# Attention scores with the low part of k on 128 partitions, and longer planned load times, in a one-core transformer block

## The chip, the cores and the metric

One core of one Trainium2 chip runs the whole kernel, one launch. The metric is the device time of that launch in microseconds. The engines are TensorE (PE, with its weight loads as PEld), VectorE (DVE), ScalarE (ACT), GpSimd (POOL) and SyncE (SP), which issues the DMAs.

## What is computed

One layer of a streaming encoder on x of 1024 x 1024: a first gated feed-forward block, a mixing block with two branches (differential attention with 8 heads, an mLSTM with 4 heads), a second feed-forward block, a final norm. The change lies in the attention branch:

```python
def diff_attention(q, k, v, lam, g_subln, lambda_init):
    q = rope(q); k = rope(k)                       # 8 heads, 2 components c, 64 wide
    s = einsum('bqhcd,bkhcd->bchqk', q, k) * Dh ** -0.5   # by blocks of 128 queries
    p = softmax(where(key_chunk <= query_chunk, s, -inf))
    a = p[:, 0] - lam * p[:, 1]
    o = einsum('bhqk,bkhd->bqhd', a, v)
    return rmsnorm(o, g_subln) * (1.0 - lambda_init)
```

## The kernel before

All matmuls are made of float32r parts: a number is split into a high part, the float32r rounding (a cast on ScalarE), and a low part, the rest (a subtraction on VectorE). A product is high x high, high x low and low x high: three matmuls (`mm3`, lines 264 to 266). Weights come in units of 128 x 1024 (512 KB): a DMA into a raw buffer, the cast to `wh` on ScalarE, the subtraction to `wl` on VectorE.

The stages follow each other: first feed-forward block; projections; mLSTM and attention (attention from some 1200 to 1880 us), both with dense projections put between their steps; merge; second feed-forward block.

In the attention stage the head's q, k and v come back from DRAM. `Q` holds the high part of q in partitions 0 to 63 and the low part in 64 to 127. `Kh` holds the high part of k in both halves, so one matmul over 128 rows gives (q high + q low) x k high (line 1551). `Kl` holds the low part of k in partitions 0 to 63, and the second matmul, over 64 rows, gives q high x k low into the same bank (line 1552). There are 192 such pairs: for 8 heads, 2 components and 8 blocks of queries, in pieces of up to 512 keys. Each head is loaded in four quarters j (`load`, lines 1499 to 1510): two DMAs for `Q`, two for `Kh`, one for `Kl`. `Kh` and `Kl` have one buffer, so a head's K is asked for when the head before has all its scores.

The order of the stage is planned by the class `Flow` (lines 55 to 152), a small event simulation that runs while the program is built. Work comes as generators. A step "P" is work on TensorE with a planned cost, "A" one on ScalarE, "D" one on VectorE; "wait" lets planned time pass, "take" and "give" hold buffers, "need" and "set" are flags. Each instruction is written into its engine's list at the moment that the plan reaches it, and each engine works through its list in order. Where no step for TensorE is ready, `chunk` gives a piece of dense work: projections of q and k (`qp`, `job_qk`), of gates (`gp`, `job_g`) and of the mLSTM's output (`ab`, `job_b`). A matmul of scores is planned by `sc_time` (line 1533): 0.227 us for 512 columns, 0.12 for 256, for both matmuls of a pair.

A load is planned as a "wait" between its issue and the step that uses it. `self.lead` (line 165) is that time for a unit of weights (`unit_ahead`, lines 242 to 259: raw buffer, DMA, wait, cast, subtraction, raw buffer free; two raw buffers), for the inputs of the output projections (`load_y`, line 1205) and for a head's normed output (`merged`, line 1695). `loads` waits 3.0 for the first quarter of a head and 1.0 for each other, `loads_v` 3.5 for v. Other planned times, as the 6.0 for stores of rotated q and k, stay out of the change.

Of the kernel before, what the change touches and what calls it, by code (L numbers as in the profile page):

```python
# [11 lines left out]
F32 = mybir.dt.float32  # L12
# [31 lines left out]
class Halves:  # L44


    def __init__(self, tiles):
        self.tiles = tiles
# [105 lines left out]
class Net:  # L154
    def __init__(self, ctx, tc, aps, dbg):
        self.ctx, self.tc, self.nc, self.a, self.dbg = ctx, tc, tc.nc, aps, dbg
        nc = self.nc
        e = ctx.enter_context
        self.const = e(tc.tile_pool(name="const", bufs=1))
        self.wraw = e(tc.tile_pool(name="wraw", bufs=2))  # L160
        self.whl = e(tc.tile_pool(name="whl", bufs=4))
        self.up = e(tc.tile_pool(name="up", bufs=1))
        self.tmp = e(tc.tile_pool(name="tmp", bufs=6))
        self.uid = 0
        self.flow, self.lead = None, 5.0
        c = self.const
        self.vec = c.tile([P, NVEC], F32, name="vec")
        nc.sync.dma_start(out=self.vec, in_=aps["vec"])
        self.ones = c.tile([P, P], F32, name="ones")
        nc.vector.memset(self.ones, 1.0)  # L170
        self.zeros = c.tile([P, 64], F32, name="zeros")
        nc.gpsimd.memset(self.zeros, 0.0)
        self.onz = c.tile([P, 16], F32, name="onz")
        nc.vector.memset(self.onz, 0.0)
        nc.vector.memset(self.onz.rearrange("p (a b) -> p a b", b=2)[:, :, 0:1], 1.0)
        self.ident = c.tile([P, P], F32, name="ident")
        make_identity(nc, self.ident)
        self.epsc = c.tile([P, 1], F32, name="epsc")
        nc.vector.memset(self.epsc, EPS)
        self.mod = [c.tile([P, 8], F32, name=f"mod{g}") for g in range(9)]  # L180
        self.sc = [c.tile([P, 8], F32, name=f"sc{g}") for g in range(3)]
        self.new_u()
# [1009 lines left out]
    def load_y(self, n, src):  # L1192
        nc = self.nc
        ns = slice(n * NW, n * NW + NW)
        if n not in self.y:
            self.y[n] = [[self.u_tile(c, k, n) for c in "hl"] for k in range(KT)]
        done = []
        for k in range(KT):
            hi, lo = self.y[n][k]
            nc.sync.dma_start(out=lo.bitcast(F32), in_=src[k][:, ns])  # L1200
            if self.flow is None:
                self.split_in(hi, lo)
            else:
                def chain(k=k, hi=hi, lo=lo):
                    yield "wait", self.lead + 0.7 * k
                    yield "A", 0.62, lambda: nc.scalar.copy(hi, lo.bitcast(F32))
                    yield "D", 0.69, lambda: nc.vector.tensor_sub(lo, lo.bitcast(F32), hi.bitcast(F32))
                    if k == KT - 1:
                        done.append(1)
                self.flow.spawn(self.flow.now, chain())  # L1210
        return done if self.flow is not None else [1]
# [274 lines left out]
    def stage_attn(self, dense):  # L1486
        nc, tc = self.nc, self.tc
        nlam, gcol = self.lam[:, 2:3], self.lam[:, 3:4]
        with tc.tile_pool(name="a1", bufs=1) as a1, tc.tile_pool(name="a2", bufs=2) as a2, \
# [5 lines left out]
            qs, kh, kl = (a1.tile([P, 2, T], F32R, name=self.nm(c), tag=c) for c in ("Q", "Kh", "Kl"))  # L1495
# [3 lines left out]
            def load(hd, j):  # L1499

                part = slice(j * 256, j * 256 + 256)
                src = [[d[x].rearrange("c x r t -> (x r) c t")[:, :, part] for d in self.qkd[hd]] for x in range(2)]
                for r in range(2):
                    rows = slice(64 * r, 64 * r + 64)
                    nc.sync.dma_start(out=qs[rows, :, part].bitcast(F32), in_=src[0][r])
                yield "need", ("scored", hd - 1, 3)
                for r in range(2):
                    rows = slice(64 * r, 64 * r + 64)
                    nc.sync.dma_start(out=kh[rows, :, part].bitcast(F32), in_=src[1][0])
                nc.sync.dma_start(out=kl[0:64, :, part].bitcast(F32), in_=src[1][1])  # L1510

            def load_v(hd):
                v = [a2.tile([P, 8, P], F32R, name=self.nm("av"), tag=f"av{i}", bufs=1) for i in range(2)]
# [4 lines left out]
            def loads(hd):  # L1518
                for n in range(NH):
                    yield "need", ("qk in", hd, n)  # L1520
                for j in range(4):
                    yield "need", ("scored", hd - 1, j)
                    yield from load(hd, j)
                    yield "wait", 3.0 if j == 0 else 1.0
                    yield "set", ("qk", hd, j)

            def loads_v(hd):
                yield "need", ("valued", hd - 1)
                load_v(hd)
                yield "wait", 3.5  # L1530
                yield "set", ("v", hd)

            def sc_time(W):
# [2 lines left out]
            def score(hd, j, i, c, a):  # L1536
                qb = 2 * j + i
                W = qb * P + P
                yield "need", ("qk", hd, j)
                if hd or j or i or c:  # L1540
                    yield "need", ("begun", *self.prev[hd, j, i, c])
                yield "take", "sc"
                yield "set", ("begun", hd, j, i, c)
                x = {}

                def dots():
                    x["ps"] = ps = psA.tile([P, T], F32, name=self.nm("sc"), tag="sc")
                    for o in range(0, W, NW):
                        ks = slice(o, min(W, o + NW))
                        ql = qs[:, c, qb * P:qb * P + P]  # L1550
                        nc.tensor.matmul(ps[:, ks], ql, kh[:, c, ks], start=True, stop=False)
                        nc.tensor.matmul(ps[:, ks], ql[0:64], kl[0:64, c, ks], start=False, stop=True)  # L1552

                def top():
                    if c == 0:
                        a[i] = {"lr": a2.tile([P, 4], F32, name=self.nm("lr"), tag="lr", bufs=6)}
                    nc.vector.memset(x["ps"][0:64, W - 64:W], -3.0e38)
                    nc.vector.reduce_max(a[i]["lr"][:, 2 + c:3 + c], x["ps"][:, 0:W], axis=AX.X, negate=True)  # L1558

                def power():  # L1560
                    lr = a[i]["lr"]
                    a[i][c] = a2.tile([P, T], F32, name=self.nm("p"), tag=f"p{c}", bufs=self.p0 if c == 0 else 2)
                    nc.scalar.activation(a[i][c][:, 0:W], x["ps"][:, 0:W], AF.Exp, bias=lr[:, 2 + c:3 + c],  # L1563
                                         accum_out=lr[:, c:c + 1])

                def shares():
                    lr = a[i]["lr"]
                    nc.vector.reciprocal(lr[:, 0:2], lr[:, 0:2])
                    nc.vector.tensor_scalar(lr[:, 1:2], lr[:, 1:2], nlam, None, op0=ALU.mult)

                def scaled():
                    nc.scalar.activation(a[i][0][:, 0:W], a[i][0][:, 0:W], AF.Copy, scale=a[i]["lr"][:, 0:1])

                def joined():
                    p0, p1, lr = a[i][0], a[i][1], a[i]["lr"]
                    nc.vector.scalar_tensor_tensor(p0[:, 0:W], p1[:, 0:W], lr[:, 1:2], p0[:, 0:W],
                                                   op0=ALU.mult, op1=ALU.add)
                    if i == 0:
                        nc.gpsimd.memset(p0[:, W:W + P], 0.0)

                yield "P", sc_time(W), dots
                if (i, c) == (1, 1):
                    yield "set", ("scored", hd, j)
                yield "D", 0.27 + 1.04e-3 * W, top
                yield "take", f"p{c}"
                yield "A", 0.4 + 0.84e-3 * W, power
                yield "give", "sc"
                if c == 0:
                    return
                yield "D", 0.37, shares  # L1590
                yield "A", 0.31 + 0.74e-3 * W, scaled
                yield "D", 0.2 + 1.06e-3 * W, joined
                yield "give", "p1"
                yield "set", ("p", hd, j, i)
# [95 lines left out]
            def merged(hd):  # L1690

                yield "need", ("b", 0)
                hi, lo = self.y[0][hd]
                nc.sync.dma_start(out=lo.bitcast(F32), in_=self.yad[hd][:, 0:NW])
                yield "wait", self.lead
                yield "A", 0.62, lambda: nc.scalar.copy(hi, lo.bitcast(F32))
                yield "D", 0.69, lambda: nc.vector.tensor_sub(lo, lo.bitcast(F32), hi.bitcast(F32))

# [221 lines left out]
```

## Time and profile before

| | us |
|---|---|
| median of 3 runs | 2755.39 (2755.03 to 2756.48) |
| the profiled execution | 2758.73 |
| its span, first to last instruction | 2757.0 |
| TensorE busy in the span | 2664.2 |
| VectorE, ScalarE busy | 1791.4, 1270.3 |
| the attention stage, 1200 to 1880 us of the span | 680.0 |

Busy time of TensorE is that of overlapping matmuls, whose ends are modelled; the spacing of their starts is what the list costs. A wait in the profile is idle time of an engine with the instruction that ended it. The chain of waits is the work that ended last, followed back step by step.

### The profile page before, as it was taken

Reading aid. Unit: us, or ns where it says so; the run is one execution under the profiler, and the core shown is the slowest. Engines: PE = TensorE matmul, PEld = TensorE weight load, DVE = VectorE, ACT = ScalarE, POOL = GpSimd, SP = SyncE. Lnnn points to the kernel's source line nnn. Section 1 sums busy time; section 2 is a strip of 40 time slices with the busy share of each in tenths; the row PEclk is TensorE's granted clock in tenths of the full one; section 3 lists DMA queues with packets and bytes.
Section 4 is the critical chain, followed back from the end, with each engine's and each line's share of the span. In section 5 each row is a group of like instructions: output and inputs, shape, how many; then the busy total and the mean of one; then the engine's idle time right before and its main releaser. Section 6 shows DMA issues by size and latency. Waiting matters only on the chain.

```text
span 2757.0 us, 35214 instructions
## 1 busy us (share of the span) xinstructions
PE 2664.2 (97%) x12704; PEld 2163.6 (78%) x12704; DVE 1791.4 (65%) x3214; ACT 1270.3 (46%) x2374; POOL 22.5 (1%) x85
## 2 busy tenths in 40 slices
PE   6999999999999899989999998999999999999998
PEld 4888888788778799977777776767888888888886
DVE  8977777768775465546555553555556866666967
ACT  6433334446443455544555543555346333334443
POOL 0000000000000000000000000000000000000000
PEclk8999999999999999999999999999999999999999
DMA  7443446634786544243334333356642332335533
GB/s 263 159 137 119 145 129 235 224 92 144 248 333 207 191 157 157 93 157 102 130 124 138 127 114 103 117 185 216 235 153 69 122 110 88 112 113 193 170 94 122
DMA packets 210183, 422.45 MB, mean 153 GB/s; under 512 B 21348, under 2 KB 79144, under 8 KB 210008
## 3 DMA queue, kind: packets, MB, share of 16 engines
q1 hardware_dynamic: 210008, 420.19, 46.3%
q8 instruction: 100, 1.64, 0.2%
q14 instruction: 75, 0.61, 0.1%
HBM read 297.05 MB, written 123.06 MB: 152 GB/s over the span
## 4 chain that ended last, share of the span: by engine, by line
PE 85%; DMA 7%; ACT 3%; DVE 2%; issue 1%; SPq 1%; POOL 0%; DVEq 0%; ACTq 0%; POOLq 0%
PE gu L264 10%; PE gu L266 10%; PE gu L265 10%; PE acc L264 5%; PE acc L265 5%; PE acc L266 5%; DMA wr<-win 2%; PE sc L1552 2%; PE dn L264 2%; PE dn L265 2%; PE dn L266 2%; PE ab L264 2%; PE ab L266 2%; PE ab L265 2%; PE gp L264 2%; PE qp L264 2%
## 5 line engine op out<-in xcount | busy, mean ns | idle before, releaser
L264 PE MATMUL gu<-uh,wh 128*128 128x512 f32 x800 | 314.8, 393 | 10.6 <-ACT uh L333 8.8
L265 PE MATMUL gu<-ul,wh 128*128 128x512 f32 x800 | 314.0, 392 | 1.5 <-DVE ul L334 1.5
L266 PE MATMUL gu<-uh,wl 128*128 128x512 f32 x800 | 313.6, 392 | 0.0
L264 PE MATMUL acc<-uh,wh 128*128 128x512 f32 x616 | 241.5, 392 | 0.0
L265 PE MATMUL acc<-ul,wh 128*128 128x512 f32 x616 | 240.1, 390 | 0.5 <-DVE ul L270 0.5
L266 PE MATMUL acc<-uh,wl 128*128 128x512 f32 x616 | 239.8, 389 | 0.0
L269 ACT CAST wh<-wr 128x512 fp32r<-128x512 f32 x228 | 134.0, 619 | 202.9 <-PE gu L265 129.9
L264 PEld LDWEIGHTS gu<-uh,wh 128*128 128x128 f32 x800 | 151.4, 189 | 46.2 <-ACT uh L333 10.4
L265 PEld LDWEIGHTS gu<-ul,wh 128*128 128x128 f32 x800 | 151.5, 189 | 34.0 <-DVE ul L334 2.4
L266 PE MATMUL gu<-ut,wl 128*128 128x512 f32 x456 | 177.4, 389 | 0.0
L264 PE MATMUL gu<-ut,wh 128*128 128x512 f32 x456 | 177.4, 389 | 0.0
L265 PE MATMUL gu<-ut,wh 128*128 128x512 f32 x456 | 177.4, 389 | 0.0
L266 PEld LDWEIGHTS gu<-uh,wl 128*128 128x128 f32 x800 | 151.5, 189 | 32.3 <-DVE wl L231 0.8
L270 DVE TENSOR_TENSOR wl<-wr,wh 128x512 fp32r<-128x512 f32 x228 | 153.8, 687 | 0.1
L269 ACT CAST uh<-hr 128x512 fp32r<-128x512 f32 x154 | 95.5, 620 | 99.8 <-PE acc L266 74.1
L1563 ACT ACTIVATE p<-sc,lr 128x256 f32<-128x256 f32 (+7 forms) x128 | 95.1, 743 | 91.0 <-DVE lr L1558 81.0
L264 PEld LDWEIGHTS acc<-uh,wh 128*128 128x128 f32 x616 | 115.6, 188 | 26.3 <-issue 2.2
L265 PEld LDWEIGHTS acc<-ul,wh 128*128 128x128 f32 x616 | 115.6, 188 | 25.6 <-DVE ul L270 1.3
L266 PEld LDWEIGHTS acc<-uh,wl 128*128 128x128 f32 x616 | 115.6, 188 | 24.1
L230 ACT CAST wh<-wr 128x1024 fp32r<-128x1024 f32 x75 | 78.8, 1050 | 120.4 <-PE wo L265 45.0
L549 ACT COPY t<-gu 128x512 f32<-128x512 f32 x114 | 66.8, 586 | 135.4 <-PE gu L266 131.2
L219 DVE SCALAR_TENSOR_TENSOR ada<-ada,crep 128x1024 f32<-128x1024 f32 x72 | 87.7, 1222 | 61.2 <-DMA ada<-wada 61.2
(332 smaller groups left out, 6631.2 us busy)
## 6 DMA issues: line engine op xcount, KB each, us to landing
ada<-wada SPq DMA_DIRECT2D x72, 512.0 KB
wr<-win SPq DMA_DIRECT2D x48, 512.0 KB
wr<-w1gu SPq DMA_DIRECT2D x44, 512.0 KB
wr<-w2gu SPq DMA_DIRECT2D x44, 512.0 KB
wr<-wab SPq DMA_DIRECT2D x32, 512.0 KB
qkh<-ro SPq DMA_DIRECT2D x32, 256.0 KB
Kh<-qkh SPq DMA_DIRECT2D x64, 128.0 KB
g<-t SPq DMA_DIRECT2D x32, 256.0 KB
```

The costliest lines, as they stand in the source:

```text
L219: nc.vector.scalar_tensor_tensor(raw, raw, 1.0, self.crep, op0=ALU.mult, op1=ALU.mult, accum_out=self.mod[g][:, k:k + 1])
L230: nc.scalar.copy(hi, raw)
L264: mm(ps, w[0], x[0], start=start, stop=False, skip_group_check=again)
L265: mm(ps, w[0], x[1], start=False, stop=False, skip_group_check=again)
L266: mm(ps, w[1], x[0], start=False, stop=stop, skip_group_check=again)
L269: (eng or self.nc.scalar).copy(hi, src)
L270: self.nc.vector.tensor_sub(lo, src, hi.bitcast(F32))
L549: nc.scalar.copy(t, ps)
L1552: nc.tensor.matmul(ps[:, ks], ql[0:64], kl[0:64, c, ks], start=False, stop=True)
L1563: nc.scalar.activation(a[i][c][:, 0:W], x["ps"][:, 0:W], AF.Exp, bias=lr[:, 2 + c:3 + c], accum_out=lr[:, c:c + 1])
```

## The change

`Kl` is filled in both halves of the partitions, with one DMA more per quarter (two for `Kh`, two for `Kl`, in turn), and the second matmul of a pair contracts over 128 rows: it gives (q high + q low) x k low. The planned time of a weight load goes from 5.0 to 7.0, of Q and K from 3.0 and 1.0 to 4.5 and 2.0, of v from 3.5 to 6.0, of a head's output from 5.0 to 6.0; that of `load_y` stays at 5.0, now as a number of its own.

```diff
--- before.py
+++ after.py
@@ -162,7 +162,7 @@
         self.up = e(tc.tile_pool(name="up", bufs=1))
         self.tmp = e(tc.tile_pool(name="tmp", bufs=6))
         self.uid = 0
-        self.flow, self.lead = None, 5.0
+        self.flow, self.lead = None, 7.0
         c = self.const
         self.vec = c.tile([P, NVEC], F32, name="vec")
         nc.sync.dma_start(out=self.vec, in_=aps["vec"])
@@ -1202,7 +1202,7 @@
                 self.split_in(hi, lo)
             else:
                 def chain(k=k, hi=hi, lo=lo):
-                    yield "wait", self.lead + 0.7 * k
+                    yield "wait", 5.0 + 0.7 * k
                     yield "A", 0.62, lambda: nc.scalar.copy(hi, lo.bitcast(F32))
                     yield "D", 0.69, lambda: nc.vector.tensor_sub(lo, lo.bitcast(F32), hi.bitcast(F32))
                     if k == KT - 1:
@@ -1506,8 +1506,8 @@
                 yield "need", ("scored", hd - 1, 3)
                 for r in range(2):
                     rows = slice(64 * r, 64 * r + 64)
-                    nc.sync.dma_start(out=kh[rows, :, part].bitcast(F32), in_=src[1][0])
-                nc.sync.dma_start(out=kl[0:64, :, part].bitcast(F32), in_=src[1][1])
+                    for x, o in ((kh, src[1][0]), (kl, src[1][1])):
+                        nc.sync.dma_start(out=x[rows, :, part].bitcast(F32), in_=o)
 
             def load_v(hd):
                 v = [a2.tile([P, 8, P], F32R, name=self.nm("av"), tag=f"av{i}", bufs=1) for i in range(2)]
@@ -1521,13 +1521,13 @@
                 for j in range(4):
                     yield "need", ("scored", hd - 1, j)
                     yield from load(hd, j)
-                    yield "wait", 3.0 if j == 0 else 1.0
+                    yield "wait", 4.5 if j == 0 else 2.0
                     yield "set", ("qk", hd, j)
 
             def loads_v(hd):
                 yield "need", ("valued", hd - 1)
                 load_v(hd)
-                yield "wait", 3.5
+                yield "wait", 6.0
                 yield "set", ("v", hd)
 
             def sc_time(W):
@@ -1549,7 +1549,7 @@
                         ks = slice(o, min(W, o + NW))
                         ql = qs[:, c, qb * P:qb * P + P]
                         nc.tensor.matmul(ps[:, ks], ql, kh[:, c, ks], start=True, stop=False)
-                        nc.tensor.matmul(ps[:, ks], ql[0:64], kl[0:64, c, ks], start=False, stop=True)
+                        nc.tensor.matmul(ps[:, ks], ql, kl[:, c, ks], start=False, stop=True)
 
                 def top():
                     if c == 0:
@@ -1692,7 +1692,7 @@
                 yield "need", ("b", 0)
                 hi, lo = self.y[0][hd]
                 nc.sync.dma_start(out=lo.bitcast(F32), in_=self.yad[hd][:, 0:NW])
-                yield "wait", self.lead
+                yield "wait", 6.0
                 yield "A", 0.62, lambda: nc.scalar.copy(hi, lo.bitcast(F32))
                 yield "D", 0.69, lambda: nc.vector.tensor_sub(lo, lo.bitcast(F32), hi.bitcast(F32))
```

The planned times move instructions on all engines of the stage. Two places:

SyncE, the end of the first head's loads (`Q`, `Kh`, `Kl` from the head's `qkh` and `qkl`), with the units of weights `wr` behind them. Before:

```order
L1505 DMA Q_11949<-qkh_329 64x2x256
L1505 DMA Q_11949<-qkl_330 64x2x256
L1509 DMA Kh_11950<-qkh_329 64x2x256 x2
L1510 DMA Kl_11951<-qkl_330 64x2x256
L1505 DMA Q_11949<-qkh_329 64x2x256
L1505 DMA Q_11949<-qkl_330 64x2x256
L1509 DMA Kh_11950<-qkh_329 64x2x256 x2
L1510 DMA Kl_11951<-qkl_330 64x2x256
L253 DMA wr_12084<-win 128x1024
L253 DMA wr_12250<-win 128x1024
L253 DMA wr_12252<-win 128x1024
```

Now, from the last quarter on:

```order
L1505 DMA Q_11949<-qkh_329 64x2x256
L1505 DMA Q_11949<-qkl_330 64x2x256
L1510 DMA Kh_11950<-qkh_329 64x2x256
L1510 DMA Kl_11951<-qkl_330 64x2x256
L1510 DMA Kh_11950<-qkh_329 64x2x256
L1510 DMA Kl_11951<-qkl_330 64x2x256
L253 DMA wr_12098<-win 128x1024
L253 DMA wr_12265<-win 128x1024
L253 DMA wr_12267<-win 128x1024
```

Each quarter is six issues instead of five, and the three units of weights stand behind them as before.

ScalarE, deep in the stage, a cast of weights (L255) among exponentials (L1563), the scaling of p (L1572), the norm of a head's output (L1680, L1683), evictions of dense work (L1177) and the high part of a transposed p (L1618). Before:

```order
L1563 ACTIVATE p_15611,lr_15572<-sc_15598,lr_15572 128x512
L255 CAST wh_15580<-wr_15589 128x1024
L1572 ACTIVATE p_15593<-p_15593,lr_15572 128x512
L1680 ACTIVATE osq_15559<-oss_15625,epsc 128x512
L1683 ACTIVATE osq_15559<-osq_15559 128x512
L1177 COPY t_15653<-gp_15582 128x512
```

Now, the same unit of weights:

```order
L1563 ACTIVATE p_15612,lr_15586<-sc_15596,lr_15586 128x512
L1177 COPY t_15626<-gp_15529 128x512
L1572 ACTIVATE p_15592<-p_15592,lr_15586 128x512
L1680 ACTIVATE osq_15573<-oss_15643,epsc 128x512
L1683 ACTIVATE osq_15573<-osq_15573 128x512
L1618 CAST ah_15666<-pt_15651 128x512
L1563 ACTIVATE p_15669,lr_15656<-sc_15645,lr_15656 128x640
L255 CAST wh_15615<-wr_15624 128x1024
L1177 COPY t_15689<-gp_15617 128x512
```

The cast stood right behind the second exponential of a block; now it comes five instructions later, behind the scaling, both steps of the norm, a cast of a transposed p and the next block's exponential.

## Rows read from the trace of the kernel before

**Rows 1.** The page, busy time: engine, us, share of the span, instructions.
```profile
PE 2664.2 (97%) x12704; PEld 2163.6 (78%) x12704; DVE 1791.4 (65%) x3214; ACT 1270.3 (46%) x2374; POOL 22.5 (1%) x85
```

**Rows 2.** Busy time by stretch, the attention stage: us and instructions by engine, clock, DMA share.
```profile
1200.00:1880.00 680.00, 642.73 (x2861) 476.75 (x2860) 374.20 (x723) 337.19 (x648) 6.45 (x32) 0.96 0.41 132
```

**Rows 3.** Timeline of TensorE, 512 columns: start us, us, engine, line, out<-in, shapes.
```profile
1242.39 0.39 PE L266 MATMUL qp<-uh,wl 128*128 128x512 f32 x1
1242.62 0.39 PE L1551 MATMUL sc<-Kh,Q 128*128 128x512 f32 x1
1242.94 0.50 PE L1552 MATMUL sc<-Kl,Q 64*128 64x512 f32 x1
1243.37 0.50 PE L264 MATMUL qp<-uh,wh 128*128 128x512 f32 x1
1243.70 0.39 PE L265 MATMUL qp<-ul,wh 128*128 128x512 f32 x1
1243.93 0.39 PE L266 MATMUL qp<-uh,wl 128*128 128x512 f32 x1
```

**Rows 4.** The same timeline, a pair of 256 columns, and two dense matmuls of 256.
```profile
1215.31 0.28 PE L1551 MATMUL sc<-Kh,Q 128*128 128x256 f32 x1
1215.82 0.50 PE L264 MATMUL qp<-uh,wh 128*128 128x512 f32 x1
1216.16 0.40 PE L265 MATMUL qp<-ul,wh 128*128 128x512 f32 x1
...
1236.98 0.28 PE L264 MATMUL po<-ah,av 128*128 128x256 f32 x1
1237.10 0.28 PE L265 MATMUL po<-al,av 128*128 128x256 f32 x1
```

**Rows 5.** Line 1552 by form; its and L1551's weight loads: busy, mean ns | idle before.
```profile
L1552 PE MATMUL sc<-Kl,Q x192: 323/492/792, 1206.0 to 1869.1; 64*128 64x512 f32 x96, 64*128 64x128 f32 x32, 64*128 64x256 f32 x32, 64*128 64x384 f32 x32
...
L1551 PEld LDWEIGHTS sc<-Kh,Q 128*128 128x128 f32 x192 | 36.8, 191 | 36.2 <-issue 18.9 <-ACT p L1563 13.2 <-DMA qkh<-ro 0.2
L1552 PEld LDWEIGHTS sc<-Kl,Q 64*128 64x128 f32 x192 | 35.9, 187 | 47.6 <-issue 42.8 <-DMA qkh<-ro 0.3
```

**Rows 6.** Waits of TensorE in the stage: us in total, times, longest us.
```profile
PE sc L1551 <- ACT p L1563: 11.5, 4, 4.6
PE qp L264 <- ACT wh L255: 8.0, 1, 8.0
PE pt L1614 <- DVE p L1576: 6.9, 1, 6.9
...
PE sc L1551 <- DMA Kh<-qkh: 2.2, 1, 2.2
```

**Rows 7.** Waits of ScalarE for DMA in the stage, the same columns.
```profile
ACT wh L255 <- DMA wr<-win: 53.3, 12, 10.1
...
ACT qa L1109 <- DMA qkl<-qa: 22.6, 4, 7.8
ACT t L1230 <- DMA t<-g: 14.6, 2, 13.0
```

**Rows 8.** Timeline of ScalarE behind a late cast of weights.
```profile
1659.39 1.04 ACT L255 CAST wh<-wr 128x1024 fp32r<-128x1024 f32 x1 [10.14 <-DMA wr<-win]
1660.34 0.72 ACT L1572 ACTIVATE p<-p,lr 128x512 f32<-128x512 f32 x1
1661.66 0.63 ACT L1683 ACTIVATE osq<-osq 128x512 f32<-128x512 f32 x1
```

**Rows 9.** Chain of waits at the first head, two of its pieces: start us, us, what.
```profile
1218.18 0.61 SPq L1505
...
1224.75 3.94 DMA wr<-win
```

**Rows 10.** The same chain later: the weights of the late cast.
```profile
1646.80 12.57 DMA wr<-win
```

**Rows 11.** Timeline of TensorE at the first head.
```profile
1220.53 0.69 PE L1551 MATMUL sc<-Kh,Q 128*128 128x384 f32 x1 [3.05 <-ACT p L1563]
```

## The prediction

> **What bounds the kernel now.** I read the page first, then the stretch of the attention stage, then the matmuls of the scores one by one, then who waits for whom. TensorE is busy for 97% of the span [rows 1]; in the stage that the change touches it is busy for 642.7 of 680 us, while VectorE and ScalarE are busy for about half and the DMA engines for 0.41 [rows 2]. So the stage ends when TensorE's list ends: 680 us are 643 of matmuls, spaced as they come, and 37 of waits. Two things can be gained, spacing and waits.
>
> Spacing first. In [rows 3] two dense matmuls of 512 columns start 0.23 us apart, and a dense one is followed by the score matmul on `Kh` after the same 0.23, although output, weights and moving operand all change. From there it goes wrong: `Kh` to `Kl` takes 0.32, `Kl` to the next dense matmul 0.43, that one to its successor 0.33. Start to start that is 1.08 us for three matmuls of 512 columns, against 3 x 0.23 = 0.69: a loss of 0.39. At 256 columns [rows 4] it is 0.85 us for two of 256 and one of 512 where the pace is 0.12 + 0.12 + 0.23 = 0.47: a loss of 0.38. The loss does not grow with the columns, so it belongs to the passage between the two kinds of matmul, and the only thing that sets `Kl` apart is its `64*128`: 64 rows of weights where all others have 128 [rows 5]. The weight loads say the same: one load takes 187 ns (64 rows) or 191 ns (128 rows), no difference, but their unit stood idle for 42.8 us before the loads for `Kl` and 18.9 us before those for `Kh` with nothing to wait for but the issue [rows 5].
>
> Waits second. TensorE's longest are for ScalarE's exponentials (11.5 us), for one weight cast (8.0) and for one VectorE join (6.9) [rows 6]. Behind them stands ScalarE, which works its list in order and waited for DMA: 53.3 us for weights in 12 casts, 22.6 us for stores that must leave the buffer `qa`, 14.6 us for `g` [rows 7]. In [rows 8] a cast comes 10.14 us late, and the scaling of p behind it, which needs no weights, with it; TensorE lost 6.9 us there.
>
> **The change, part by part.**
>
> *128 rows for the low part.* The matmuls stay 192 + 192, with the same columns. The product of both low parts is now in the sum, at no cost in columns. What goes is the passage: 96 pairs of 512 columns at 0.39 (37.4 us) and 64 pairs of 384 and 256 at 0.38 (24.3 us) make 61.7. For the 32 pairs of 128 columns no row shows what two full matmuls of that width cost, between half of the 0.12 of 256 columns and all of it; I take the same 0.38 (12.2 us) and would lose 0.11 of it each, 3.5 us, at the other end. Sum: **74 us less** on TensorE, all of it on the path, since these are gaps between matmuls that wait for nothing. Bounds: 62, the idle time of the weight loads (42.8 + 18.9), and 77, 192 x 0.40. Where this goes, ScalarE and VectorE are late next.
>
> *32 more loads of 128 KB for `Kl`.* 4.2 MB on the stage's 680 us x 132 GB/s = 90 MB; DMA engines that are busy for 0.41 [rows 2] take that beside the rest. On SyncE's queue each issue takes 0.61 us [rows 9]. A refill of one head grows from 20 issues to 24, by 2.4 us, and what is queued behind are the weights. At the first head TensorE waits for just such weights (8.0 us, issue at 1224.75 after the burst that began at 1218.18): three of its four quarters now stand ahead of them with one issue more each, **2 us more**. At later heads I cost it at nothing: weights for the next jobs were asked for well ahead, and dense matmuls cover; if the cover were gone it would be 7 x 2.4 = 17 us.
>
> *More time for weights (5 to 7).* The planner sets the cast later in ScalarE's and VectorE's lists, by 2 us of planned work. In the rows of the order the cast that came 10.14 us late now stands behind the scaling, both steps of osq, a cast of p's transpose and an exponential. The first three took 1660.34 to 1662.29, 2.0 us [rows 8], and they no longer stand behind the weights. But today's plan runs slow: the planner counts a pair at the dense pace, so TensorE needs 74 us more than planned (680 against 606, some 12%), so the 5 us are in truth about 5.6. The net gift is 1.4 us for each of the 12 late casts, **17 us of ScalarE's waiting**.
>
> *Q and K 3.0 to 4.5 and 1.0 to 2.0, v 3.5 to 6.0, the merge 5 to 6; `load_y` stays at 5.* TensorE waited once for `Kh`, for 2.2 us, in no row for v. These shift scores and outputs behind dense matmuls in the list. I cost them at nothing as long as dense jobs are left. Without that cover the price is 7 heads x (1.5 + 2.5) = 28 us.
>
> *The waits that grow.* Stores out of `qa` and loads of `g` keep their planned time, and each loses the 12% that the slow pace gave: some 0.7 us on 6 waits, 4 us. Weights that take over 12 us [rows 10] stay late against any plan here. So ScalarE would wait for DMA 53.3 + 22.6 + 14.6 - 17 + 4 = 78 us instead of 90. Today TensorE feels 37 of 90, four tenths, because its own slow pace hides the rest. With the pace as planned I take a larger share, 55%, 43 us: **6 us more**. Ends: the share of today (31 us, 6 less) and everything felt (78 us, 41 more).
>
> Sum: -74 + 2 + 6 = -66 us. The profiled execution took 2758.7 us, span 2757.0; that gives 2692.7. It stands 3.3 us above the median, so for the median 2689, which I round to **2690**.
>
> **The rivals.**
>
> *A. Rows do not matter.* The pair would be slow for another cause (the same Q loaded twice, a fresh accumulation) and stays so. Then only 17 us of ScalarE's waits go, four tenths felt, -7, with +2: 2755.4 - 5 = 2750. For it: both loads last the same time. Against: a dense matmul to `Kh` changes all operands for 0.23, and the loss comes also after `Kl`. The Trainium skill (TensorE: Matmul & The Clock Gate, the table under "Why this matters for your kernels") has a rule on its side: a matmul of 32 rows takes as long as one of 128. By that rule the sum would hold only the waits. The trace agrees for the loads' duration and not for the spacing. Another page (TensorEngine Tiling (Array Packing), "Key Properties") says that a change of the tiling mode drains the engine. Chance 0.05.
>
> *B. SyncE's refill becomes the bound.* Faster scores bring each head's end nearer to its refill of 24 issues (24 x 0.61 = 14.6 us), and weights issued behind it come when TensorE has nothing left. The first head shows the price: 11 us (the 8.0 and a 3.05 just before, [rows 11]). If each of the seven others lost that and 2.4 for the longer burst, it is 7 x 13.4 = 94, with 2 more: 2755.4 - 74 + 96 = 2777, **slower**. It decides at a loss of 72 / 7 = 10.3 us a head. Against: in 680 us SyncE's issue held TensorE once, where the stage has no work yet. Chance 0.04.
>
> *C. ScalarE's late DMA is felt in full.* The 78 us all come through: -74 + 2 + 41 = -31, 2724. For it: it works in order, and TensorE has few banks to run ahead. Against: today only four tenths come through. Chance 0.09.
>
> **How the numbers follow.** My forecast has 0.82. Its own ends: 77 saved and 6 us of waits less (2755.4 - 83 + 2 = 2674, and a few us below if the late weights go altogether), or 62 saved and 25 us more waiting (2720). The range goes from 2668 to 2726, which takes in C and leaves out A and B. A measurement of this kernel tells about 0.2% (5.5 us) from no change. Faster: forecast and C, 0.91; the same: A's 2750 lies at that edge, 0.04; slower: B and a part of A that is worse than I priced it, 0.05.
>
> **What would show it.** Right: `Kl` is `128*128`, both score matmuls start at 0.23 us per 512 columns, and the idle time "issue" before the loads of these lines (61.7 us) falls below 15. The stage is some 65 us shorter, with the stretches before and after it as they are. ScalarE's waits for weights fall, those for `qa` and `g` do not. Wrong: the pair keeps 0.32 and 0.43 (A); TensorE waits for weights behind the refill at each head (B); TensorE's waits in the stage are over 60 us (C).

## The result and the profile after

| | before | changed kernel |
|---|---|---|
| median, us | 2755.93 (4 runs, 2755.03 to 2761.04) | 2680.9 (4 runs, 2678.2 to 2684.37) |
| ratio to before | | 0.9725 (95%: 0.9708 to 0.9742) |
| the profiled execution, us | 2758.73 | 2680.27 |
| its span, us | 2757.0 | 2678.6 |

The time lies inside the range, 9 us below the forecast of 2690. (The kernel before has one run more here than when the forecast was made.) The span is 78.4 us shorter, and all of it is in the attention stage. Behind the start of its last score there are 888 us before (2757.0 - 1869.1, [rows 5]) and 888 after (2678.6 - 1791.0), and the stretch up to 1200 us has the same 1160 us of TensorE work. Busy time by stretch, the stage of the changed kernel, which answers to [rows 2] (us and instructions by engine, clock, DMA share; both stages end 11 us behind the start of the last score):

```profile
1200.00:1802.00 602.00, 568.98 (x2867) 475.74 (x2866) 374.02 (x724) 336.46 (x647) 6.46 (x32) 0.96 0.47 156
```

TensorE's busy time fell from 642.7 to 569.0 us, by 73.7, and its waits from 37.3 to 33.0, by 4.3. VectorE and ScalarE do the same work in a shorter stage. Over the whole span TensorE is busy for 2590.4 us, again 97%.

Where the 73.7 us went is seen in the timeline of TensorE, a pair of 512 columns, against [rows 3]:

```profile
1242.27 0.39 PE L266 MATMUL qp<-uh,wl 128*128 128x512 f32 x1
1242.50 0.39 PE L1551 MATMUL sc<-Kh,Q 128*128 128x512 f32 x1
1242.72 0.39 PE L1552 MATMUL sc<-Kl,Q 128*128 128x512 f32 x1
1242.95 0.39 PE L264 MATMUL qp<-uh,wh 128*128 128x512 f32 x1
1243.18 0.39 PE L265 MATMUL qp<-ul,wh 128*128 128x512 f32 x1
```

Start to start it is 0.22, 0.23 and 0.23 us: from the first score matmul to the second dense one 0.68 us, where it was 1.08. Line 1552 by form, and the weight loads of both lines (busy, mean ns | idle before), against [rows 5]:

```profile
L1552 PE MATMUL sc<-Kl,Q x192: 274/389/654, 1208.4 to 1791.0; 128*128 128x512 f32 x96, 128*128 128x128 f32 x32, 128*128 128x256 f32 x32, 128*128 128x384 f32 x32
```

```profile
L1551 PEld LDWEIGHTS sc<-Kh,Q 128*128 128x128 f32 x192 | 36.9, 192 | 16.2 <-ACT p L1572 7.8 <-issue 1.2 <-ACT p L1563 0.4
L1552 PEld LDWEIGHTS sc<-Kl,Q 128*128 128x128 f32 x192 | 36.9, 192 | 8.3 <-issue 1.8
```

A load lasts 192 ns as before, but the idle time "issue" is 1.2 and 1.8 us where it was 18.9 and 42.8. The waits of TensorE and of ScalarE in the stage (us in total, times, longest), against [rows 6] and [rows 7]:

```profile
PE qp L264 <- ACT qa L1109: 12.4, 2, 7.6
PE sc L1551 <- ACT p L1572: 7.4, 1, 7.4
PE pt L1614 <- DVE al L1622: 5.8, 4, 3.7
PE qp L264 <- ACT wh L255: 3.4, 1, 3.4
```

```profile
ACT wh L255 <- DMA wr<-win: 23.9, 12, 5.3
ACT qa L1109 <- DMA qkl<-qa: 22.8, 4, 10.2
ACT t L1230 <- DMA t<-g: 14.9, 4, 6.3
```

ScalarE's waiting for weights fell from 53.3 to 23.9 us; that for `qa` and `g` stayed.

### The profile page after: what moved, and what is told of

It reads as the page before. It is cut to its first block, busy times and chain, and to the rows that moved or that the text cites. A ratio compares the mean times of both kernels' runs of the same rounds, so it can differ in the third digit from the quotient of the medians.

```text
span 2678.6 us, 35281 instructions
## 1 busy us (share of the span) xinstructions
PE 2590.4 (97%) x12704; PEld 2162.5 (81%) x12704; DVE 1789.2 (67%) x3214; ACT 1269.8 (47%) x2374; POOL 22.5 (1%) x85
## 4 chain that ended last, share of the span: by engine, by line
PE 86%; DMA 5%; DVE 4%; ACT 2%; issue 1%; SPq 1%; POOL 0%; DVEq 0%; ACTq 0%; POOLq 0%
PE gu L264 10%; PE gu L266 10%; PE gu L265 10%; PE acc L264 5%; PE acc L265 5%; PE acc L266 5%; PE dn L264 2%; PE dn L266 2%; PE dn L265 2%; PE gp L264 2%; PE gp L266 2%; PE gp L265 2%; PE ab L264 2%; PE ab L266 2%; PE ab L265 2%; PE qp L264 2%
## 5 line engine op out<-in xcount | busy, mean ns | idle before, releaser
L264 PEld LDWEIGHTS gu<-uh,wh 128*128 128x128 f32 x800 | 151.4, 189 | 46.0 <-ACT uh L333 10.4
L1563 ACT ACTIVATE p<-sc,lr 128x256 f32<-128x256 f32 (+7 forms) x128 | 95.1, 743 | 95.7 <-DVE lr L1558 82.0
```

Source lines behind the costliest of these rows:

```text
L264: mm(ps, w[0], x[0], start=start, stop=False, skip_group_check=again)
```

## The experiments

My theory: the saved spacing is that of the passage between 64 and 128 rows of weights, and the longer planned times are worth little (in the forecast, 17 us of ScalarE's waiting, half of it felt). Rivals: rows do not matter and the planned times carry the gain; or the extra loads eat much of it. Where two kernels ran in different groups of runs I compare their ratios to before; 0.1% is 2.8 us.

**Only the rows.** `Kl` loaded twice and contracted over 128 rows, all planned times as before (against the changed kernel):

```diff
-        self.flow, self.lead = None, 7.0
+        self.flow, self.lead = None, 5.0
-                yield "wait", 4.5 if j == 0 else 2.0
+                yield "wait", 3.0 if j == 0 else 1.0
-                yield "wait", 6.0
+                yield "wait", 3.5
-                yield "wait", 6.0
+                yield "wait", self.lead
```

> The second half of Kl is loaded and the low matmul contracts over 128 rows; all planned times stay as in the kernel before. If the gain is the passage between 64-row and 128-row weights (my theory), nearly all of it is here: some 74 us off TensorE's list. My price for the shorter planned weight times is 17 us more of ScalarE's waiting for weights, of which TensorE feels about half, so 2681 + 9 = 2690 us. If the planned times carry the gain, this kernel stays at 2750 us or above. If they are worth nothing, it gives 2681 us.

Measured 2722.5 us, 0.9886 (0.9867 to 0.9906). A miss by 32 us: the rows alone do not bring the result. TensorE was busy for 576.1 us of the stage and waited for 67.9; ScalarE waited 71.6 us for weights in 15 casts, where it was 53.3 before.

**Only the planned times**, the counterpart: the changed kernel with one load of `Kl` and 64 rows:

```diff
-                    for x, o in ((kh, src[1][0]), (kl, src[1][1])):
-                        nc.sync.dma_start(out=x[rows, :, part].bitcast(F32), in_=o)
+                    nc.sync.dma_start(out=kh[rows, :, part].bitcast(F32), in_=src[1][0])
+                nc.sync.dma_start(out=kl[0:64, :, part].bitcast(F32), in_=src[1][1])
-                        nc.tensor.matmul(ps[:, ks], ql, kl[:, c, ks], start=False, stop=True)
+                        nc.tensor.matmul(ps[:, ks], ql[0:64], kl[0:64, c, ks], start=False, stop=True)
```

> Only the planned times change (weights 7.0, Q and K 4.5 and 2.0, v 6.0, the merge 6.0); Kl has 64 rows as before. My theory: 2750 us, some 5 us less than before, since TensorE's slow pace hides most of the late loads already. If the planned times carry the gain: 2690 us or less. If they move TensorE's waits elsewhere without gain: 2756 us.

Measured 2731.5 us, 0.9916 (0.9901 to 0.9931), a second miss on the same side: they save 23 us (0.84%) even at TensorE's slow pace. The stage, and ScalarE's waiting for weights:

```profile
1200.00:1853.00 653.00, 635.82 (x2880) 474.11 (x2879) 374.28 (x723) 337.58 (x647) 6.46 (x32) 0.98 0.42 138
```

```profile
ACT wh L255 <- DMA wr<-win: 10.4, 6, 5.2
```

TensorE waits for 17.2 us where it was 37.3, its clock in the stage is 0.98 of full where it was 0.96, and ScalarE waits 10.4 us for weights where it was 53.3.

**The changed kernel with 64 rows**, its order and its loads untouched:

```diff
-                        nc.tensor.matmul(ps[:, ks], ql, kl[:, c, ks], start=False, stop=True)
+                        nc.tensor.matmul(ps[:, ks], ql[0:64], kl[0:64, c, ks], start=False, stop=True)
```

> The changed kernel with its order, its planned times and its 32 extra loads, and one thing undone: the low matmul uses 64 rows again. If the passage between 64 and 128 rows costs 0.38 us a pair, TensorE's list grows by 74 us, and the time is 2681 + 74 = 2755 us less what the slow pace hides of the 33 us of waits (some 10): 2745 to 2755 us. If rows do not matter and the gain comes from order or times: 2681 us. Start to start the pair goes back to 0.32 and 0.43 us.

Measured 2737.9 us, 0.9941 (0.9926 to 0.9956): that one operand loses 57 us by the medians, 60 by the ratios, and the time is 7 us below the low end that I had given. TensorE waits for 23.3 us, 9.7 less, as I had said; what falls short is the busy time, 635.2 us, 66 more and not 74, at a granted clock of 0.98 where the changed kernel has 0.96. That rows do not matter has fallen.

**Passages grouped**, on the kernel before:

```diff
-                    for o in range(0, W, NW):
-                        ks = slice(o, min(W, o + NW))
-                        ql = qs[:, c, qb * P:qb * P + P]
-                        nc.tensor.matmul(ps[:, ks], ql, kh[:, c, ks], start=True, stop=False)
-                        nc.tensor.matmul(ps[:, ks], ql[0:64], kl[0:64, c, ks], start=False, stop=True)
+                    ql = qs[:, c, qb * P:qb * P + P]
+                    for low in range(2):
+                        for o in range(0, W, NW):
+                            ks = slice(o, min(W, o + NW))
+                            if low:
+                                nc.tensor.matmul(ps[:, ks], ql[0:64], kl[0:64, c, ks], start=False, stop=True)
+                            else:
+                                nc.tensor.matmul(ps[:, ks], ql, kh[:, c, ks], start=True, stop=False)
```

> The kernel before, 64 rows, with one thing moved: where a block of queries has two pieces of keys, both matmuls on Kh come first and then both on Kl, so that 64 of the 128 groups of scores have one passage to 64 rows and back instead of two. If the loss belongs to the passage: 64 x 0.39 = 25 us less, 2730 us. If it belongs to each 64-row matmul by itself: no change, 2755 us.

Measured 2737.6 us, 0.9943 (0.9925 to 0.9962): 16 us less (10 to 21) for the same 192 matmuls over 64 rows, short of the 25 that I had expected. The profiled execution was the fastest of the four (2734.9 us). Its stage, to 11 us behind the start of the last score:

```profile
1200.00:1855.50 655.50, 615.53 (x2854) 470.12 (x2853) 375.22 (x724) 336.55 (x647) 6.43 (x32) 0.96 0.42 137
```

TensorE's busy time is 615.5 us, 27 less than before, about the 25 expected; 2.7 us came back as waits (40.0 for 37.3), and much of the rest of the shortfall is the place of the two profiled executions among their runs (this one 2.6 us below its median, that of before 3.3 above). The same group of scores, 512 and 128 columns with a dense matmul of 512 behind it, in three timelines of TensorE. Two passages, in the changed kernel with 64 rows:

```profile
1338.26 0.39 PE L1551 MATMUL sc<-Kh,Q 128*128 128x512 f32 x1
1338.57 0.50 PE L1552 MATMUL sc<-Kl,Q 64*128 64x512 f32 x1
1339.00 0.33 PE L1551 MATMUL sc<-Kh,Q 128*128 128x128 f32 x1
1339.26 0.33 PE L1552 MATMUL sc<-Kl,Q 64*128 64x128 f32 x1
1339.51 0.50 PE L264 MATMUL gp<-uh,wh 128*128 128x512 f32 x1
1339.86 0.40 PE L265 MATMUL gp<-ul,wh 128*128 128x512 f32 x1
```

One passage, grouped (each row holds a matmul of 512 and one of 128 columns):

```profile
1331.76 0.45 PE L1555 MATMUL sc<-Kh,Q 128*128 128x512 f32 x2
1332.14 0.56 PE L1553 MATMUL sc<-Kl,Q 64*128 64x512 f32 x2
1332.63 0.50 PE L264 MATMUL gp<-uh,wh 128*128 128x512 f32 x1
1332.97 0.39 PE L265 MATMUL gp<-ul,wh 128*128 128x512 f32 x1
```

None, in the changed kernel:

```profile
1247.03 0.39 PE L1551 MATMUL sc<-Kh,Q 128*128 128x512 f32 x1
1247.26 0.39 PE L1552 MATMUL sc<-Kl,Q 128*128 128x512 f32 x1
1247.48 0.22 PE L1551 MATMUL sc<-Kh,Q 128*128 128x128 f32 x1
1247.54 0.28 PE L1552 MATMUL sc<-Kl,Q 128*128 128x128 f32 x1
1247.65 0.45 PE L264 MATMUL qp<-uh,wh 128*128 128x512 f32 x1
1247.94 0.39 PE L265 MATMUL qp<-ul,wh 128*128 128x512 f32 x1
```

From the first score matmul to the second dense one it is 1.60, 1.21 and 0.91 us. A second passage to 64 rows and back costs 0.39 us here, the first 0.30, and one passage can hold two matmuls of 64 rows.

**Zeros instead of the second copy.** `Kl`'s second half is filled with zeros once, and the 32 loads are gone; the low matmul keeps its 128 rows. What it leaves out against the changed kernel is the product of both low parts, which the kernel before left out too:

```diff
+            for c in range(2):
+                for o in range(0, T, NW):
+                    nc.vector.tensor_copy(kl[64:128, c, o:o + NW].rearrange("p (c t) -> p c t", t=64),
+                                          self.zeros[64:128].rearrange("p (o t) -> p o t", o=1).broadcast_to([64, 8, 64]))
-                    for x, o in ((kh, src[1][0]), (kl, src[1][1])):
-                        nc.sync.dma_start(out=x[rows, :, part].bitcast(F32), in_=o)
+                    nc.sync.dma_start(out=kh[rows, :, part].bitcast(F32), in_=src[1][0])
+                nc.sync.dma_start(out=kl[0:64, :, part].bitcast(F32), in_=src[1][1])
```

> The changed kernel, but Kl's second half is filled with zeros once (four VectorE instructions at the start of the stage) and its 32 extra loads are gone; the low matmul still contracts over 128 rows. If only the number of rows matters, the pair keeps 0.23 us per 512 columns and the time is that of the changed kernel, 2681 us, less the 2 us by which I priced the extra issues at the first head: 2679 us. If the extra loads cost more than I priced (the SyncE queue as a growing bound): 2665 to 2675 us. If zeros or a half-empty operand slowed the array: over 2700 us.

Measured 2668.1 us, 0.9687 (0.9673 to 0.9700), outside the interval of the changed kernel: it beats both. The extra loads cost 10 us (0.38% of 2756), 13 by the medians, where I had priced 2. Against the kernel with only the planned times (0.9916), which differs in nothing but the 64 rows and the zeros, 128 rows are worth 2.29%, 63 us, and TensorE's busy time falls by 73.1 us at the same clock of 0.98. The stage and TensorE's waits:

```profile
1200.00:1787.00 587.00, 562.73 (x2851) 470.68 (x2850) 372.29 (x720) 335.11 (x643) 6.46 (x32) 0.98 0.46 153
```

```profile
PE qp L264 <- ACT qa L1109: 10.3, 2, 6.7
PE sc L1555 <- ACT p L1567: 6.5, 1, 6.5
PE pt L1618 <- DVE al L1626: 2.9, 2, 1.8
PE qp L264 <- ACT wh L255: 2.1, 1, 2.1
```

Waits are 24.3 us instead of 33.0, each of the four groups smaller, and the work itself takes 562.7 instead of 569.0 at a clock of 0.98 instead of 0.96.

**Which planned time.** The changed kernel with Q, K and v put back to 3.0, 1.0 and 3.5:

```diff
-                    yield "wait", 4.5 if j == 0 else 2.0
+                    yield "wait", 3.0 if j == 0 else 1.0
-                yield "wait", 6.0
+                yield "wait", 3.5
```

> 128 rows and the planned time of weights at 7.0 (and the merge at 6.0); Q, K and v back at 3.0, 1.0 and 3.5. The planned times together are worth 2722 - 2681 = 41 us with 128 rows. If it is the weights (my theory, since ScalarE's waits for them fell from 53 to 24 us): 2681 to 2690 us. If it is Q, K and v: 2710 us or more.

And with the weights put back to 5.0:

```diff
-        self.flow, self.lead = None, 7.0
+        self.flow, self.lead = None, 5.0
```

> The other half: 128 rows, weights back at 5.0, Q and K at 4.5 and 2.0, v at 6.0. By my theory 2710 to 2720 us, with ScalarE waiting for weights as in the kernel with rows only. If Q, K and v carry the planned times' gain: 2681 to 2690 us.

Measured 2690.5 us, 0.9766 (0.9752 to 0.9779), and 2712.6 us, 0.9848 (0.9835 to 0.9861). From the kernel with rows only (0.9886), the weights' time takes 1.20%, 33 us, and the time of Q, K and v 0.38%, 10 us; both together 1.61%. Each of the two keeps the merge's 6.0, so what that 1 us of planned time is worth stands in both and was not measured by itself. Apart from that they add up, and three quarters are the weights'. With their time alone ScalarE waits for weights 30.5 us where it was 71.6, and TensorE's waits fall from 67.9 to 46.3. The second part I had priced at nothing. What is late without it (waits of TensorE, the kernel with the weights' time only):

```profile
PE qp L264 <- ACT qa L1109: 16.4, 2, 15.8
...
PE sc L1551 <- DMA Kh<-qkh: 4.6, 1, 4.6
```

TensorE waits 4.6 us for the first head's `Kh`, and 16.4 for the copies into `qa` where it was 12.4. Its longest wait, 15.8 us, ends with a store out of `qa` that SyncE issues here and in the changed kernel at:

```profile
1300.77 0.55 SPq L1131 DMA_DIRECT2D qkl<-qa  x1
```

```profile
1294.25 0.55 SPq L1131 DMA_DIRECT2D qkl<-qa  x1
```

Here the last two quarters of a head's refill (issued from 1289.62 to 1300.01) stand ahead of the store in SyncE's list; in the changed kernel they stand behind it (from 1294.85 on).

**The stores that the change left at 6.0**, planned at 10.0 in the changed kernel:

```diff
-        return [("take", "rb")] + steps[:8] + [("give", "rb")] + steps[8:] + [("wait", 6.0), ("give", "rot")] + done
+        return [("take", "rb")] + steps[:8] + [("give", "rb")] + steps[8:] + [("wait", 10.0), ("give", "rot")] + done
```

> The changed kernel, and the planned time of the stores of rotated q and k, which the change left at 6.0, goes to 10.0. ScalarE waited 22.8 us for those stores, and TensorE 12.4 us behind them, in two waits near 1302 and 1320 us. If the planned time is what is short there: 2668 to 2675 us. If the plan only moves the wait to TensorE or to another buffer: 2681 us or more.

Measured 2678.1 us, 0.9723 (0.9709 to 0.9736): no difference. ScalarE waits less for the stores, 13.3 us where it was 22.8, but TensorE's two waits behind them stay (12.0 us for 12.4), and a new one of 3.7 for an exponential has come. With zeros as well, both edits together:

> Zeros in Kl's second half, and 10.0 instead of 6.0 for the stores of rotated q and k. The stores' time alone was worth 3 us on the changed kernel. If both add: 2665 us. If the stores' waits at 1296 and 1312 us stay, since they come from the refill of K that stands ahead of them, not from the plan: 2668 us.

2670.9 us, 0.9686 (0.9673 to 0.9700): again none beside 0.9687. TensorE's two waits fall from 10.3 to 8.5 us, and one of 6.5 for the first head's `Kh` has come. More planned time for the stores gains nothing that could be measured.

**Issues or bytes.** The kernel with zeros, and 32 small loads:

```diff
+                nc.sync.dma_start(out=kl[64:128, :, j * 256:j * 256 + 8].bitcast(F32), in_=src[1][1][:, :, 0:8])
```

> The kernel with zeros in Kl's second half, and the 32 extra loads back as issues with almost no bytes: each brings 8 of the 256 columns, 4 KB instead of 128 KB. The zeros were worth 13 us over the changed kernel. If the issues on SyncE's queue (24 a head instead of 20) cost that: 2681 us. If the 4 MB of bytes cost it: 2668 us. In between: both.

2676.7 us, 0.9706 (0.9693 to 0.9720), in between, and its interval meets both others. How the cost is shared between the issues and the bytes stays open.

**Weights at 9.0**, with zeros:

```diff
-        self.flow, self.lead = None, 7.0
+        self.flow, self.lead = None, 9.0
```

> Zeros in Kl's second half, and the planned time of weights at 9.0. ScalarE still waits 19 us for weights in 11 casts. If the planned time is still short: 2660 to 2665 us. If two raw buffers of weights now limit (each is held 2 us longer) or other waits take over: 2668 us or more.

2666.6 us, 0.9670 (0.9657 to 0.9683). The interval meets that of the kernel with zeros; a gain beyond 7.0 is not shown.

**The rows with nothing else**: the kernel before with zeros in `Kl`'s second half (the four lines above) and 128 rows, no extra load, no planned time changed:

```diff
-                        nc.tensor.matmul(ps[:, ks], ql[0:64], kl[0:64, c, ks], start=False, stop=True)
+                        nc.tensor.matmul(ps[:, ks], ql, kl[:, c, ks], start=False, stop=True)
```

> The kernel before with one thing changed for TensorE alone: the low matmul contracts over 128 rows, the second half of Kl being zeros written once; no extra load, all planned times as before. Spacing falls by some 72 us. If late loads take back about as much as in the kernel with rows only and its 32 loads (30 us of new waits), less the 13 us that the loads cost: 2709 us. If the loads were what ate the gain there: 2690 us or less.

2710.0 us, 0.9825 (0.9811 to 0.9838), as expected. The stage, TensorE's waits and ScalarE's waits for DMA:

```profile
1200.00:1833.00 633.00, 577.13 (x2848) 481.51 (x2847) 374.27 (x723) 335.92 (x646) 6.43 (x32) 0.95 0.43 142
```

```profile
PE sc L1555 <- ACT p L1567: 16.3, 4, 7.9
PE pt L1618 <- DVE p L1580: 9.6, 3, 8.2
PE qp L264 <- ACT wh L255: 8.4, 1, 8.4
```

```profile
ACT wh L255 <- DMA wr<-win: 59.3, 13, 10.5
...
ACT qa L1109 <- DMA qkl<-qa: 22.5, 4, 7.4
...
ACT t L1230 <- DMA t<-g: 17.1, 2, 15.4
```

The spacing is the good one, but waits have gone from 37.3 to 55.9 us, and ScalarE waits 59.3 us for weights in 13 casts.

The change taken apart by ratios, in this order: rows alone -1.75% (48 us), planned times on top -1.38% (38 us), the 32 loads +0.38% (10 us). The sizes depend on the order. Rows are worth 48 us with the old planned times and 63 with the new ones; the planned times 23 us with 64 rows and 38 with 128. The 32 loads cost 17 us with 128 rows and the old times (0.9886 beside 0.9825), 10 with the new times, and 7 with 64 rows and the new times (0.9941 beside 0.9916, intervals that just meet).

## Why the prediction was right, and where it was not

*The passage* was right in kind and size: 74 us forecast, 73.7 us less busy time, and 73.1 where nothing but the rows differs and the clock is the same (only the planned times, beside zeros). Putting 64 rows back in the changed kernel brings 66 us back, and grouping 64 of the passages takes away 27. The 0.38 us taken for a pair of 128 columns was a little high: in the one case shown a pair of 512 and one of 128 lose 0.69 us together (1.60 for 0.91), some 0.30 for the 128, 2.6 us less over 32 pairs. Rival A has fallen. The Trainium skill's rule on its side (TensorE: Matmul & The Clock Gate, "Why this matters for your kernels", few rows cost as much as 128) holds for the loads' duration, 187 and 192 ns, and says nothing of the passage. The Trainium skill's page TensorEngine Tiling (Array Packing), "Key Properties", by which a change of tiling mode drains the engine, agrees with 0.3 to 0.4 us per passage that do not grow with the columns; that a drain is what happens inside, no run here shows.

*"All of it on the path"* was wrong as the step stands: of 74 us, rows alone bring 48. The rest returns as 18.6 us more waiting of TensorE (55.9 for 37.3) and, as I read it, as a lower clock (577.1 us busy for 569.0, below): 73.7 - 18.6 - 8.1 = 47. ScalarE's own waiting for DMA grew little, from 90.5 to 98.9 us; TensorE felt more of it. That the sum came within 9 us is partly luck: the rows alone brought 26 us less than their term, the 32 loads cost 8 more than theirs, and the planned times gave 38 us where 17 us of ScalarE's waiting, half of it felt, make some 9.

*More time for weights*: the mechanism was right, the term too small. I had 17 us of ScalarE's waiting; it fell by 29.4 (53.3 to 23.9). With 128 rows and the old times it was 71.6 (59.3 without the 32 loads), and from there the weights' time alone takes away 41 us, to 30.5, and, with the merge's, 33 us of the total. The step that failed is the fixed gift ("1.4 us for each of the 12 late casts"). With 64 rows, where the same rule gives 2 x 1.12 x 12 = 27 us, the waiting fell by 42.9 (53.3 to 10.4), and only 6 casts were late at all.

*Q, K and v at nothing*: wrong, 10 us with 128 rows. Without that time TensorE's waits are 13.3 us longer (46.3 for 33.0): 4.6 for the first head's `Kh`, 4.0 more behind the stores of `qa`, the rest in small ones. The longest wait behind those stores, 15.8 us, goes with the order of SyncE's list shown above: there two more quarters of a refill stand ahead of the store that the wait ends with.

*32 more loads at 2 us*: mis-sized, 10 us (7 to 17, by what else is changed). I priced the first head and called the later ones covered. Without them every group of waits shrinks (`qa` 12.4 to 10.3, the exponentials and scaling of the first head 7.4 to 6.5, the transposes 5.8 to 2.9, the first weights 3.4 to 2.1): not one place, but a little at each.

*The share that TensorE feels*: 55% was forecast, and 33.0 of 62.2 us (the three rows above and 0.6 for the weights of the output projections) is 53%; rows alone give 55.9 of 98.9 (the three rows shown there), 57%, and before it was 41%. That a TensorE at its planned pace hides less is not shown by this: in the pair that differs in rows alone, planned times and zeros, it is 45% (17.2 of 38.1) and 46% (24.3 of 52.5), and with the stores at 10.0 it is 74% (36.0 of 48.6). The share is no fixed property of the pace, and that 55% came out is luck. I expected 78 us of ScalarE's waiting and there were 62, since the weights' fell by 29.4 and not 17, and `qa` and `g` did not grow by the 4 us either. So TensorE's waits fell by 4.3 us instead of rising by 8 (6, and 2 for the loads): these 12 us are the difference between the 66 us forecast and the 78.4 by which the profiled span is shorter.

*Rivals B and C.* TensorE waits for weights once in the stage, 3.4 us at the first head, so B fell, though its grain, the price of the extra issues or bytes, was real. C needed all of ScalarE's waiting to be felt; it was half.

## What to carry to other kernels

Try to keep every matmul of a stream on the same number of rows: here an operand of 64 rows saved a load and cost 0.3 to 0.4 us for each passage there and back, and filling its second half with zeros once, which needs no load, beat both kernels (0.9687). When a list planned in advance gets faster on its bounding engine, plan its loads anew in the same step: here rows alone brought 48 of 74 us, and rows and planned times together 86 (with zeros), more than the 48 and 23 that each brought alone. Price small extra transfers beyond the one place where the profile shows them on the path: 32 loads put at 2 us cost 7 to 17.

## What was not expected of the hardware

Waits can cost more than their own length. The same matmuls took 569.0 us of busy time in the changed kernel at a granted clock of 0.96, 562.7 with zeros at 0.98, and 577.1 with rows alone at 0.95. That all of this difference is the clock is not shown. The timeline of TensorE in the changed kernel behind one of the two waits for `qa`, and the stretch by engine (the clock is the third number from the end):

```profile
1302.11 0.80 PE L264 MATMUL qp<-uh,wh 128*128 128x512 f32 x1 [7.56 <-ACT qa L1109]
1302.70 0.63 PE L265 MATMUL qp<-ul,wh 128*128 128x512 f32 x1
1303.13 0.63 PE L266 MATMUL qp<-uh,wl 128*128 128x512 f32 x1
1303.55 0.63 PE L264 MATMUL qp<-uh,wh 128*128 128x512 f32 x1
```

```profile
1302.10:1303.90 1.80, 1.79 (x4) 1.49 (x5) 1.04 (x2) 1.23 (x4) 0.00 (x0) 0.50 0.51 139
```

Before this wait of 7.56 us the granted clock was 1.00 (1290 to 1294 us) and matmuls of 512 columns started 0.23 us apart. Behind it they start 0.43 us apart at a granted clock of 0.50: the lower of the clock's two levels, 1.2 GHz for 2.4. The forecast had no term for it.
